# Where large and small tiles start in on-chip memory: pool order, a 128-byte pad, and a 192-byte shift of the swiglus' moving operand

## The chip, the core and the metric

The kernel runs on one core of a Trainium2 chip. The core has a matrix engine (TensorE, called PE in the rows; PEld is its loading of stationary operands), three other compute engines (VectorE = DVE, ScalarE = ACT, GpSimd = POOL), and a queue engine (SyncE = SP) that issues most transfers. Operands lie in SBUF, 128 partitions wide; "address" below means the byte offset inside a partition, which is the same in all of them. Matmul results go to PSUM banks. The metric is device microseconds (us) of one execution, less is better.

## What is computed

The reference is two transformer blocks of two layers each, on one sequence of 256 tokens and 1024 features, in float32. Cut to what the change touches:

```python
def swiglu(h, w_gate, w_up, w_down):
    return (jax.nn.silu(h @ w_gate) * (h @ w_up)) @ w_down

def first_block(x, mem, ...):                      # D_MODEL 1024, D_FF 2816, SEQ 256
    for layer in range(2):
        x = x + 0.5 * swiglu(rms_norm(x, ...), ...)
        x = x + (diff_stickbreak_mixer if layer == 0 else mla_mixer)(rms_norm(x, ...), ...)
        x = x + memory_cross_attention(rms_norm(x, ...), rms_norm(mem, ...), ...)
        x = x + 0.5 * swiglu(rms_norm(x, ...), ...)
    return x

def second_block(x, ...):                          # FFN_HIDDEN 2816
    for l in range(2):
        x = _layer_norm(ALPHA * x + mixers(x) @ w_out[l], ...)
        x = _layer_norm(ALPHA * x + swiglu(x, ...), ...)
    return x
```

So there are six swiglus, and they hold most of the weights.

## The kernel before, in words

**Three products for one.** Every large matrix product is done in split precision. `parted` (lines 144 to 159) takes a weight tile of 128 x 1024 floats that SP has brought to `wr`; ACT writes its rounded part `wh` (line 157), DVE the rest `wl` (line 158). Activations are split the same way into `op` (high) and `ol` (low) by `split_T` (lines 232, 233) or inside `swiglu` (lines 348, 349). A product is then wl·op + wh·ol + wh·op: three matmuls, each with a stationary operand of 128 columns of its own.

**The swiglu.** `norm_T` transposes the normalised x into tiles made by `operand(8)`: 8 blocks of 128 features, each 256 tokens wide, 4 blocks to a tile of 1024 floats, two `op` and two `ol` tiles. In the gate and up part (11 turns of 4 weight tiles of 24 matmuls: 1056 matmuls, recorded under line 467) the weights are stationary and the activations move, 256 columns a time. The product of gate and up goes to 22 further blocks (six `op` and six `ol` tiles). In the down part (`dense`, lines 195 to 219, matmuls recorded under 215, 216 and 217) the activations are stationary, 128 columns a time, and the weights move, 512 columns a time: 2 halves of 11 weight tiles of 12 matmuls, 264 in all. The last four weight tiles of the second half do not use the kept `wh` and `wl` but eight tiles of the scope, so that they can be split early (`apart`).

**Scopes and pools.** The program is a sequence of scopes: ffn, m0 (first mixer and memory attention), ffn, ffn, m1, ffn, m2, ffn2, m2, ffn2. `KEEP` tiles (`x`, `wr`, `wh`, `wl` and small gains) live through the whole program. For each scope, `SCOPES` lists tags with the number of their buffers; `scope` opens one pool for each tag in the order of the list, and the pools are laid one behind the other in SBUF. A tile of tag `s` or `ls` (any suffix) is 16 floats, 64 bytes; `b05` is 512 bytes, `b1` 1024, `b2` 2048, and `op`, `ol`, `g4`, `wh`, `wl` are 4096. So the order of the list sets every address, and the number of 64-byte tiles ahead of a large one sets where it starts within 512 bytes. The next scope lies on the same memory as the last one; a tile of it waits for the readers and writers of just those old tiles that it covers.

**Order of the work.** The instructions of an engine are put in order at build time by a scheduler that goes by priorities and by when an operand's room is free; on the chip each engine takes them in that order, and so does the SP queue. Work of the next scope (`later(-ahead)` in `norm_T`) may be moved ahead of the end of the last, as far as its room is free by then.

**m2's own projections** (`dense_T`, line 1035) are written like a swiglu's gate and up part: stationary weight slices of 128 columns from the kept `wh` and `wl`, 256 moving columns from `op` and `ol`, the same three products, recorded under line 467 too.

Of the kernel before, what the change touches and what calls it, by code (L numbers as in the profile page):

```python
# [14 lines left out]
F32 = mybir.dt.float32  # L15
F32R = mybir.dt.float32r
# [4 lines left out]
X = mybir.AxisListType.X  # L21
# [7 lines left out]
class Core:  # L29
# [4 lines left out]

    KEEP = dict(x=2, g1=4, v1=1, wr=4, wh=3, wl=2)
    SCOPES = {
        "ffn": (dict(s=10, ls=16, g4=2, b2=6, b1=6, b05=2, lb1=1, op=8, ol=8, wh=4, wl=4),
                dict(t=2, d=6)),
        "ffn2": (dict(s=10, ls=8, b2=6, b1=6, op=8, ol=8, wh=4, wl=4, g2=4),
                dict(t=3, d=5)),  # L40
        "m0": (dict(s=8, ls=10, g4=2, b2=6, lb4=4, lb2=7, lb8=1, b1=1, b05=1, chains=4, b2C0=3, sC0=4, b2C1=3, sC1=4, olK=2, sC2=4,
                     b2C3=3, sC3=4, sO=3, b2O=2, opK=2, b2C2=3, b2K=3, sK=8, lsK=2, lb2K=2, lb4K=1, op=3, ol=3),
                dict(t=1, o=1, d=2, tK="t", pC0=1, pC1=1, pC2=1, pC3=1, aC0="pC0", tC0="pC0", aC1="pC1", tC1="pC1", aC2="pC2",
                     tC2="pC2", aC3="pC3", tC3="pC3", oO="o")),
        "m1": (dict(sC2=4, ls=14, g4=2, b2=5, lb2=9, b1=3, lb4=4, lb4K=1, lb05=2, lb1=1, chains=4, b2C0=2, sC0=4, b2C1=2, sC1=3,
                     b2C2=2, s=8, b2C3=3, b05=6, sO=4, ol=4, olK=2, b2K=3, sK=8, lsK=2, lb2K=3, sC3=5, op=5, opK=2),
                dict(t=1, o=1, d=2, tK="pC0", pC0=1, pC1=1, pC2=1, pC3=1, aC0="pC0", tC0="pC0", aC1="pC1", tC1="pC1", aC2="pC2",
                     tC2="pC2", aC3="pC3", tC3="pC3", oO="o")),
        "m2": (dict(lb4R=1, s=11, op=3, ol=2, lb2N=5, lb2R0=3, lb2R1=3, b2R0=1, b2R1=1, lb4N=1, b05R=4, b05G=3, b05N=3, lb05N=2,
# [202 lines left out]
    def operand(self, nb, groups=None):  # L252


        groups = groups or [("op" + self.stream, min(4, nb - b)) for b in range(0, nb, 4)]
        V = [[self.tagged(g.replace("op", lo), dict(self.SIZES).get(g[1:3], 1024), F32R)[:, :n * 256].rearrange("p (k t) -> p k t", t=256)
              for g, n in groups] for lo in ("op", "ol")]
        at = [(i, j) for i, (g, n) in enumerate(groups) for j in range(n)]
        put = lambda h, b, m: [v[at[b][0]][:, at[b][1]:at[b][1] + m, h * 128:(h + 1) * 128] for v in V]
        get = lambda h, k: [v[at[k][0]][:, at[k][1], h * 128:(h + 1) * 128] for v in V]  # L260
        get.both = lambda k: [v[at[k][0]][:, at[k][1]] for v in V]
        get.blocks = lambda b, m: [v[at[b][0]][:, at[b][1]:at[b][1] + m] for v in V]
        return put, get
# [6 lines left out]
    def norm_T(self, xs, gain, gates=True):  # L270


        nc = self.nc
        ahead = self.AHEAD if gates else 0
        with self.later(-ahead):
            put, get = self.operand(8)
            ss = [self.t(2) for _ in range(2)]
        for i in range(2):

            with self.later(0 if i else -ahead):  # L280
                for h in range(2):
                    y = x = xs[h][:, 512 * i:512 * i + 512]
                    if gain is not None:
                        y = self.t(512)
                        nc.vector.tensor_tensor(y, x, gain[:, 512 * i:512 * i + 512], op=OP.mult)  # L285
                    self.split_T(y, 4, lambda b, m: put(h, 4 * i + b, m))
                    if gain is not None:
                        nc.scalar.activation(self.t(512), x, AF.Square, accum_out=ss[h][:, i:i + 1])
        if gain is not None:
            get.r = []  # L290
            for h in range(2):
                nc.vector.tensor_tensor(ss[h][:, :1], ss[h][:, :1], ss[h][:, 1:], op=OP.add)
                get.r.append(self.rstd(ss[h][:, :1], 1, 1.0 / 1024, 1e-6, self.l(1)))
            if gates:
                self.gate = self.pow
        return get
# [71 lines left out]
    def load_consts(self, cp):  # L368

        c = self.consts.tile([128, FIRST], F32, name="cf")  # L370
        self.nc.scalar.dma_start(c, cp[:, :FIRST])
        self.c = {k: c[:, a:a + n] for k, (a, n) in CONST_AT.items() if a < FIRST}
        self.ident = self.c["ident"]
        self.mhalf = self.c["mhalf"]
        self.ones = self.consts.tile([128, 128], F32, name="ones")
        self.nc.gpsimd.memset(self.ones, 1.0)

    def load_masks(self, cp, cb):
# [96 lines left out]
class Mix1(Core):  # L475
# [96 lines left out]
    def mixer0(self, filler):  # L572
# [23 lines left out]
        for h in range(2):  # L596
            qT["qb", h] = self.l(1024)
            self.fill(qT["qb", h], 0.0)
        V = {(n, h): self.l(512) for n in ("va", "vb") for h in range(2)}
        pair = lambda t: t.rearrange("p (b t) -> p b t", b=4)  # L600
# [32 lines left out]
        def value(n):  # L633
            return lambda h, ps: self.evac(V[n, h], ps, xT.r[h])

# [1253 lines left out]
```

## Time and profile before

| | |
|---|---|
| median of 3 runs | 2046.84 us (2044.94 to 2047.52) |
| the profiled execution, its own time | 2048.2 us |
| span of that execution in the trace | 2046.5 us |
| mean granted TensorE clock over the span | 0.989 |
| PE busy, share of the span | 1957.1 us, 96% |
| weight loads busy | 1740.0 us, 85% |
| DVE, ACT, POOL busy | 61%, 49%, 9% |
| read from HBM | 315.82 MB, 155 GB/s over the span |

Matmuls are pipelined: one lasts some 280 or 390 ns in the records, and the next starts long before it ends. What a matmul costs in a stream is therefore the step from its start to the next start, not its duration. In the stretches of the swiglus PE and PEld are busy all the time, at the full clock.

### The profile page before, as it was taken

The numbers are of one execution on the slowest core, as the hardware profiler recorded it, in microseconds if no ns is written. First come the engines' busy times: TensorE is split into PE (matmuls) and PEld (weight loads), VectorE is DVE, ScalarE is ACT, GpSimd is POOL, SyncE is SP. The second block draws the span as 40 slices with busy tenths as digits, with TensorE's granted clock in tenths as the row PEclk, the third lists the DMA queues.
The fourth block names the chain that finished last, engine by engine and source line by source line (L and its number), as shares of the span: only waits on it lengthen the run. The fifth ranks groups of instructions, "written<-read, shape, count | busy, mean of one in ns | idle before, by whom it ended". The sixth has DMA issues, their size and how long they took to land.

```text
span 2046.5 us, 34153 instructions
## 1 busy us (share of the span) xinstructions
PE 1957.1 (96%) x13548; PEld 1740.0 (85%) x13548; DVE 1257.9 (61%) x2007; ACT 1007.6 (49%) x1607; POOL 190.9 (9%) x270
## 2 busy tenths in 40 slices
PE   8999899899999998899999999998999999999998
PEld 7997678799989986777899888877998787878996
DVE  5655774666556655776666557756555667476555
ACT  4544556545444544665554445553544455444442
POOL 0000401000000000330000021311000212210000
PEclk9999899999999999999999999999999999999999
DMA  6656543456556655324466665313665655025664
GB/s 213 186 187 214 155 138 104 125 178 185 187 173 184 185 187 188 120 95 146 139 186 184 203 160 140 115 32 114 185 183 187 178 152 158 5 83 173 185 186 137
DMA packets 158640, 319.09 MB, mean 156 GB/s; under 512 B 28944, under 2 KB 49680, under 8 KB 158480
## 3 DMA queue, kind: packets, MB, share of 16 engines
q1 hardware_dynamic: 157888, 315.79, 50.2%
q8 instruction: 106, 1.74, 0.4%
q0 software_dynamic: 160, 0.52, 0.1%
q10 hardware_dynamic: 432, 0.60, 0.1%
q14 instruction: 54, 0.44, 0.1%
HBM read 315.82 MB, written 1.05 MB: 155 GB/s over the span
## 4 chain that ended last, share of the span: by engine, by line
PE 53%; DVE 3%; ACT 1%; issue 1%; DMA 1%; POOL 0%; SPq 0%; DVEq 0%; ACTq 0%; POOLq 0%
PE pd L467 23%; PE pd L216 6%; PE pd L215 6%; PE pd L217 6%; PE po L467 2%; DVE wl L158 1%; PE ppC L467 1%; PE pg L1234 1%; PE pg L467 1%; PE pr L1510 0%; PE pt L503 0%; PE pq L1510 0%; PE pq L1519 0%; PE pt L229 0%; PE pq L1515 0%
## 5 line engine op out<-in xcount | busy, mean ns | idle before, releaser
L158 DVE TENSOR_TENSOR wl<-wr,wh 128x1024 fp32r<-128x1024 f32 (+2 forms) x557 | 677.5, 1218 | 435.6 <-PE pd L467 174.6
L157 ACT ACTIVATE wh<-wr 128x1024 fp32r<-128x1024 f32 (+2 forms) x557 | 584.8, 1051 | 600.1 <-PE pd L467 291.5
L467 PE MATMUL pd<-op,wl 128*128 128x256 f32 x2320 | 656.2, 283 | 8.3 <-DVE lb2R L1310 4.5
L467 PE MATMUL pd<-ol,wh 128*128 128x256 f32 x2320 | 656.1, 283 | 0.4 <-DVE ol L233 0.3
L467 PE MATMUL pd<-op,wh 128*128 128x256 f32 x2320 | 653.9, 282 | 0.0
L467 PEld LDWEIGHTS pd<-op,wl 128*128 128x128 f32 x2320 | 438.7, 189 | 10.4 <-DVE lb2R L1310 5.0
L467 PEld LDWEIGHTS pd<-ol,wh 128*128 128x128 f32 x2320 | 439.4, 189 | 1.6 <-DVE ol L233 0.8
L467 PEld LDWEIGHTS pd<-op,wh 128*128 128x128 f32 x2320 | 439.7, 190 | 0.7 <-issue 0.7
L216 PE MATMUL pd<-wl,op 128*128 128x512 f32 (+5 forms) x984 | 378.5, 385 | 4.3 <-DVE wl L158 4.1
L217 PE MATMUL pd<-wh,op 128*128 128x512 f32 (+5 forms) x984 | 375.3, 382 | 0.0
L215 PE MATMUL pd<-wh,ol 128*128 128x512 f32 (+5 forms) x984 | 357.7, 386 | 2.8 <-DVE ol L233 1.7
L216 PEld LDWEIGHTS pd<-wl,op 128*128 128x128 f32 x984 | 186.4, 189 | 41.4 <-DVE wl L158 6.6
L215 PEld LDWEIGHTS pd<-wh,ol 128*128 128x128 f32 x984 | 185.5, 189 | 39.4 <-DVE ol L233 1.9
L217 PEld LDWEIGHTS pd<-wh,op 128*128 128x128 f32 x984 | 186.4, 189 | 35.3
L242 POOL TENSOR_TENSOR ls<-s,cf 128x1 f32<-128x1 f32 (+2 forms) x30 | 25.6, 857 | 760.6 <-DVE s L241 565.7
L345 DVE TENSOR_TENSOR b<-pd,b 128x256 f32<-128x256 f32 x132 | 56.0, 424 | 63.7 <-ACT b L344 44.0
L242 POOL TENSOR_TENSOR s<-s,cf 128x1 f32<-128x1 f32 (+2 forms) x22 | 22.3, 1017 | 444.8 <-DVE s L241 443.4
L344 ACT ACTIVATE b<-b 128x256 f32<-128x256 f32 x88 | 36.7, 417 | 46.3 <-DVE b L343 46.2
L349 DVE TENSOR_TENSOR ol<-b,op 128x512 fp32r<-128x512 f32 x66 | 45.4, 687 | 18.0 <-ACT op L348 18.0
L348 ACT ACTIVATE op<-b 128x512 fp32r<-128x512 f32 x66 | 41.7, 631 | 21.3 <-DVE b L345 20.8
L229 PE MATMUL pt<-cf,b 128*128 128x128 f32 x140 | 24.9, 310 | 26.3 <-DVE b L285 19.2
L343 DVE TENSOR_TENSOR b<-pd,lb 128x256 f32<-128x256 f32 x88 | 37.1, 421 | 16.5 <-PE pd L467 16.5
(505 smaller groups left out, 2055.8 us busy)
## 6 DMA issues: line engine op xcount, KB each, us to landing
wr<-in_ffn_gu_dram SPq DMA_DIRECT2D x264, 512.0 KB, 3.7
wr<-in_ffn_w_down_dram SPq DMA_DIRECT2D x132, 512.0 KB, 3.5
wr<-in_w_in_dram SPq DMA_DIRECT2D x45, 512.0 KB, 4.4
wr<-in_ab_w_in_dram SPq DMA_DIRECT2D x24, 512.0 KB, 3.9
wr<-in_xm_w_kv_dram SPq DMA_DIRECT2D x16, 512.0 KB, 3.5
wr<-in_w_out_dram SPq DMA_DIRECT2D x16, 512.0 KB, 3.7
wr<-in_ab_w_out_dram SPq DMA_DIRECT2D x8, 512.0 KB, 3.5
wr<-in_xm_w_q_dram SPq DMA_DIRECT2D x8, 512.0 KB, 3.9
```

The lines of the kernel that those rows point to most:

```text
L157: nc.scalar.activation(hi, raw, AF.Copy)
L158: nc.vector.tensor_tensor(lo, raw, hi.bitcast(F32), op=OP.subtract)
L215: nc.tensor.matmul(o, xl, wh[:, k], start=first, stop=False)
L216: nc.tensor.matmul(o, xh, wl[:, k], start=False, stop=False)
L217: nc.tensor.matmul(o, xh, wh[:, k], start=False, stop=last)
L242: self.pow = nc.gpsimd.tensor_tensor(r, a, self.mhalf[:, :n], op=OP.pow)
L343: nc.vector.tensor_tensor(s, ps[:, :256], R, op=OP.mult)
L344: nc.scalar.activation(s, s, AF.Silu)
L345: nc.vector.tensor_tensor(y[:, b * 256:b * 256 + 256], ps[:, 256:], s, op=OP.mult)
L348: nc.scalar.activation(hi, yv, AF.Copy)
L349: nc.vector.tensor_tensor(lo, yv, hi.bitcast(F32), op=OP.subtract)
L467: i = self.k.nc.tensor.matmul(out, lhsT, rhs, start=start, stop=stop, skip_group_check=skip)
```

## The change

It touches only where tiles lie. In the `SCOPES` of ffn, ffn2, m0 and m1 the 64-byte tags (`s...`, `ls...`) go to the end of the list; m2's list stays as it is. The constant tile `ones` is declared 128 bytes longer, so that everything behind it moves up by 128 bytes. The two `op` and two `ol` tiles of `norm_T` in ffn and ffn2 get tags of their own, `opX` and `olX`, 4608 bytes long, and their data starts 192 bytes behind the tile's start; the `op` and `ol` counts go from 8 to 6, so the number of buffers in use is as before.

```diff
     SCOPES = {
-        "ffn": (dict(s=10, ls=16, g4=2, b2=6, b1=6, b05=2, lb1=1, op=8, ol=8, wh=4, wl=4),
+        "ffn": (dict(g4=2, b2=6, b1=6, b05=2, lb1=1, opX=2, olX=2, op=6, ol=6, wh=4, wl=4, s=10, ls=16),
                 dict(t=2, d=6)),
-        "ffn2": (dict(s=10, ls=8, b2=6, b1=6, op=8, ol=8, wh=4, wl=4, g2=4),
+        "ffn2": (dict(b2=6, b1=6, opX=2, olX=2, op=6, ol=6, wh=4, wl=4, g2=4, s=10, ls=8),
                 dict(t=3, d=5)),
-        "m0": (dict(s=8, ls=10, g4=2, b2=6, lb4=4, lb2=7, lb8=1, b1=1, b05=1, chains=4, b2C0=3, sC0=4, b2C1=3, sC1=4, olK=2, sC2=4,
-                     b2C3=3, sC3=4, sO=3, b2O=2, opK=2, b2C2=3, b2K=3, sK=8, lsK=2, lb2K=2, lb4K=1, op=3, ol=3),
+        "m0": (dict(g4=2, b2=6, lb4=4, lb2=7, lb8=1, b1=1, b05=1, chains=4, b2C0=3, b2C1=3, olK=2, b2C3=3, b2O=2, opK=2, b2C2=3,
+                     b2K=3, lb2K=2, lb4K=1, op=3, ol=3, s=8, ls=10, sC0=4, sC1=4, sC2=4, sC3=4, sO=3, sK=8, lsK=2),
                 dict(t=1, o=1, d=2, tK="t", pC0=1, pC1=1, pC2=1, pC3=1, aC0="pC0", tC0="pC0", aC1="pC1", tC1="pC1", aC2="pC2",
                      tC2="pC2", aC3="pC3", tC3="pC3", oO="o")),
-        "m1": (dict(sC2=4, ls=14, g4=2, b2=5, lb2=9, b1=3, lb4=4, lb4K=1, lb05=2, lb1=1, chains=4, b2C0=2, sC0=4, b2C1=2, sC1=3,
-                     b2C2=2, s=8, b2C3=3, b05=6, sO=4, ol=4, olK=2, b2K=3, sK=8, lsK=2, lb2K=3, sC3=5, op=5, opK=2),
+        "m1": (dict(g4=2, b2=5, lb2=9, b1=3, lb4=4, lb4K=1, lb05=2, lb1=1, chains=4, b2C0=2, b2C1=2, b2C2=2, b2C3=3, b05=6, ol=4,
+                     olK=2, b2K=3, lb2K=3, op=5, opK=2, sC2=4, ls=14, sC0=4, sC1=3, s=8, sO=4, sK=8, lsK=2, sC3=5),
                 dict(t=1, o=1, d=2, tK="pC0", pC0=1, pC1=1, pC2=1, pC3=1, aC0="pC0", tC0="pC0", aC1="pC1", tC1="pC1", aC2="pC2",
                      tC2="pC2", aC3="pC3", tC3="pC3", oO="o")),
...
-        V = [[self.tagged(g.replace("op", lo), dict(self.SIZES).get(g[1:3], 1024), F32R)[:, :n * 256].rearrange("p (k t) -> p k t", t=256)
-              for g, n in groups] for lo in ("op", "ol")]
+        def room(tag, n):
+
+            at = 48 if tag[2:] == "X" else 0
+            t = self.tagged(tag, 1152 if at else dict(self.SIZES).get(tag[1:3], 1024), F32R)
+            return t[:, at:at + n * 256].rearrange("p (k t) -> p k t", t=256)
+        V = [[room(g.replace("op", lo), n) for g, n in groups] for lo in ("op", "ol")]
...
-            put, get = self.operand(8)
+            put, get = self.operand(8, [("opX", 4)] * 2 if "opX" in self.caps[0] else None)
...
-        self.ones = self.consts.tile([128, 128], F32, name="ones")
+        self.ones = self.consts.tile([128, 160], F32, name="ones")[:, :128]
```

Where operands start, as the built programs place them, in bytes within 512. "Apart" means moving start minus stationary start within 512. Slices step by 512 bytes or its multiples, so a tile's start holds for all its slices.

| matmuls | moving before | stationary before | apart before | moving after | stationary after | apart after |
|---|---|---|---|---|---|---|
| swiglus, gate and up | 0 | 384 | 128 | 192 | 0 | 192 |
| swiglus, down, kept weights | 384 | 0 | 384 | 0 | 0 | 0 |
| swiglus, down, the last four tiles | 0 | 0 | 0 | 0 | 0 | 0 |
| m2's projections (`dense_T`) | 64 | 384 | 192 | 192 | 0 | 192 |

The engines' instructions are the same in kind and number, but at the seams between scopes some stand elsewhere, since another old tile lies below. On the SP queue this is the load of the mixer's gain (`mix_norm`, 128 x 512 twice), which m0's first multiplication (line 285) needs. Near the program's start, before:

```order
L139 DMA wr_286<-in_ffn_gu_dram 128x1024
L171 DMA cp<-in_constants_dram 128x802
L171 DMA cb<-in_masks_dram 128x1608
L139 DMA wr_338<-in_ffn_gu_dram 128x1024
L139 DMA wr_368<-in_ffn_gu_dram 128x1024
```

and at the end of the first swiglu, where m0's first weights (`ab_w_in`) and the memory input are loaded, before:

```order
L132 DMA wr_2472<-in_ab_w_in_dram 128x2x512
L132 DMA wr_2490<-in_ab_w_in_dram 128x2x512
L798 DMA lb_303_2192<-in_mem_dram 128x1024
L798 DMA lb_304_2194<-in_mem_dram 128x1024
L171 DMA g_305_2196<-in_mix_norm_dram 128x512 x2
L171 DMA g_328_2259<-in_xm_mem_norm_dram 128x512 x2
```

In the changed program the load stands at the first of these places:

```order
L139 DMA wr_292<-in_ffn_gu_dram 128x1024
L171 DMA cp<-in_constants_dram 128x802
L171 DMA cb<-in_masks_dram 128x1608
L171 DMA g_305_2204<-in_mix_norm_dram 128x512 x2
L139 DMA wr_344<-in_ffn_gu_dram 128x1024
L139 DMA wr_374<-in_ffn_gu_dram 128x1024
```

It moved from behind the memory loads to the head of the program. For m1 the same load moves from the end of the third swiglu to its beginning.

On PE the place is the end of the first swiglu. Its last matmuls (here `wh_2016`, `wl_2017`), m0's first transposes (line 229, four to a row, of a gained block `b`) and m0's first projection (`ol_2201`), before:

```order
L215 MATMUL pd_1869<-wh_2016,ol_193 128x512
L216 MATMUL pd_1869<-wl_2017,op_187 128x512
L217 MATMUL pd_1869<-wh_2016,op_187 128x512
L229 MATMUL pt_2207<-cf,b_312_2205 128x128 x4
L229 MATMUL pt_2218<-cf,b_315_2216 128x128 x4
L215 MATMUL pd_2348<-wh_2352,ol_2201 128x512
L216 MATMUL pd_2348<-wl_2353,op_2199 128x512
```

In the changed program, 118 matmuls earlier:

```order
L215 MATMUL pd_1874<-wh_1896,ol_194 128x512
L215 MATMUL pd_1875<-wh_1896,ol_194 128x512
L229 MATMUL pt_2215<-cf,b_312_2213 128x128 x4
L216 MATMUL pd_1874<-wl_1897,op_188 128x512
L217 MATMUL pd_1874<-wh_1896,op_188 128x512
```

and at the swiglu's end:

```order
L215 MATMUL pd_1875<-wh_2022,ol_199 128x512
L216 MATMUL pd_1875<-wl_2023,op_193 128x512
L217 MATMUL pd_1875<-wh_2022,op_193 128x512
L229 MATMUL pt_2226<-cf,b_315_2224 128x128 x4
L215 MATMUL pd_2356<-wh_2360,ol_2209 128x512
L216 MATMUL pd_2356<-wl_2361,op_2207 128x512
```

The first four transposes moved in among the down matmuls; the second four stayed at the end. The end of the third swiglu, ahead of m1, reads alike. The split of the first four (line 232 on ACT, into an `op` tile of m0) has its new room on top of one of the `wl` tiles of the swiglu's last four weight tiles, and waits for a matmul next to the swiglu's last.

On DVE at that place the gain's multiplication of the second half of x also moves ahead, between the two updates of x (line 363 before, 368 in the changed file; line 285 before, 290 after). Before:

```order
L363 SCALAR_TENSOR_TENSOR x_65<-pd_1868,ls_178,x_65 128x512
L363 SCALAR_TENSOR_TENSOR x_66<-pd_1869,ls_179,x_66 128x512
L285 TENSOR_TENSOR b_312_2205<-x_65,g_305_2196 128x512
L285 TENSOR_TENSOR b_315_2216<-x_66,g_305_2196 128x512
L285 TENSOR_TENSOR b_318_2227<-x_65,g_305_2196 128x512
L285 TENSOR_TENSOR b_321_2238<-x_66,g_305_2196 128x512
```

and in the changed program:

```order
L368 SCALAR_TENSOR_TENSOR x_65<-pd_1874,ls_184,x_65 128x512
L290 TENSOR_TENSOR b_318_2235<-x_65,g_305_2204 128x512
L297 TENSOR_TENSOR s_2211<-s_2211 128x1
L241 TENSOR_SCALAR s_2259<-s_2211 128x1
L368 SCALAR_TENSOR_TENSOR x_66<-pd_1875,ls_185,x_66 128x512
L290 TENSOR_TENSOR b_321_2246<-x_66,g_305_2204 128x512
L233 TENSOR_TENSOR ol_2209<-pt_2215,op_2207 128x4x128
```

The multiplications of the first half (b_312, b_315) have moved some 15 instructions further up.

## Rows read from the trace of the kernel before

**Rows 1.** Page, parts 1 and 4: busy time of PE; chain that ended last.

```profile
span 2046.5 us, 34153 instructions
PE 1957.1 (96%) x13548; PEld 1740.0 (85%) x13548; DVE 1257.9 (61%) x2007; ACT 1007.6 (49%) x1607; POOL 190.9 (9%) x270
...
PE 53%; DVE 3%; ACT 1%; issue 1%; DMA 1%; POOL 0%; SPq 0%; DVEq 0%; ACTq 0%; POOLq 0%
```

**Rows 2.** Page, part 5: one of three groups of line 467 (count; busy, mean ns).

```profile
L467 PE MATMUL pd<-op,wl 128*128 128x256 f32 x2320 | 656.2, 283 | 8.3 <-DVE lb2R L1310 4.5
```

**Rows 3.** Windows in gate and up parts: us; busy (x) by engine; PEclk, DMA share, GB/s.

```profile
1005.40:1124.60 119.20, 119.20 (x1007) 119.20 (x1006) 72.42 (x94) 60.24 (x75) 0.00 (x0) 1.00 0.60 182
1422.70:1548.20 125.50, 125.50 (x1048) 125.50 (x1048) 66.84 (x74) 60.17 (x75) 0.00 (x0) 1.00 0.58 177
```

**Rows 4.** Timeline of PE in a gate and up part, first and last rows.

```profile
1049.82 0.28 PE L467 MATMUL pd<-ol,wh 128*128 128x256 f32 x1
...
1060.49 0.28 PE L467 MATMUL pd<-ol,wh 128*128 128x256 f32 x1
```

**Rows 5.** Timeline of PE in m2's projections, first and last rows.

```profile
1213.58 0.28 PE L467 MATMUL pd<-ol,wh 128*128 128x256 f32 x1
...
1224.13 0.28 PE L467 MATMUL pd<-ol,wh 128*128 128x256 f32 x1
```

**Rows 6.** Timeline of PE in the first down part, kept weights, first and last rows.

```profile
149.70 0.39 PE L216 MATMUL pd<-wl,op 128*128 128x512 f32 x1
...
160.39 0.40 PE L216 MATMUL pd<-wl,op 128*128 128x512 f32 x1
```

**Rows 7.** The same, on the last four weight tiles; then that stretch's window.

```profile
192.45 0.40 PE L217 MATMUL pd<-wh,op 128*128 128x512 f32 x1
...
203.11 0.39 PE L216 MATMUL pd<-wl,op 128*128 128x512 f32 x1
...
192.70:203.30 10.60, 10.60 (x48) 8.81 (x47) 4.42 (x4) 5.24 (x10) 0.00 (x0) 1.00 0.86 288
```

**Rows 8.** Timeline of all engines where the first swiglu ends and m0 begins.

```profile
203.34 0.39 PE L217 MATMUL pd<-wh,op 128*128 128x512 f32 x1
...
203.77 0.75 DVE L363 SCALAR_TENSOR_TENSOR x<-pd,ls,x 128x512 f32<-128x512 f32 x1 [4.69 <-PE pd L217]
204.58 0.80 SPq L171 DMA_DIRECT2D g<-in_mix_norm_dram  x2
...
208.42 2.54 DVE L285 TENSOR_TENSOR b<-x,g 128x512 f32<-128x512 f32 x4 [3.90 <-DMA g<-in_mix_norm_dram]
...
209.26 1.09 PE L229 MATMUL pt<-cf,b 128*128 128x128 f32 x4 [5.53 <-DVE b L285]
...
210.38 0.60 ACT L232 ACTIVATE op<-pt 128x512 fp32r<-128x512 f32 x1 [5.05 <-PE pt L229]
...
211.21 0.68 DVE L233 TENSOR_TENSOR ol<-pt,op 128x512 fp32r<-128x512 f32 x1
...
211.94 1.11 PE L229 MATMUL pt<-cf,b 128*128 128x128 f32 x4 [1.60 <-DVE ol L233]
...
212.71 0.77 PE L215 MATMUL pd<-wh,ol 128*128 128x512 f32 x1
```

**Rows 9.** Timeline of PE where the third swiglu ends and m1 begins.

```profile
795.92 0.39 PE L217 MATMUL pd<-wh,op 128*128 128x512 f32 x1
801.53 1.09 PE L229 MATMUL pt<-cf,b 128*128 128x128 f32 x4 [5.22 <-DVE b L285]
804.03 1.11 PE L229 MATMUL pt<-cf,b 128*128 128x128 f32 x4 [1.41 <-DVE s L241]
804.80 0.77 PE L215 MATMUL pd<-wh,ol 128*128 128x512 f32 x1
```

**Rows 10.** Windows behind those two seams (columns as in rows 3).

```profile
207.50:217.70 10.20, 6.84 (x20) 5.40 (x21) 7.58 (x26) 3.81 (x7) 5.06 (x5) 0.50 0.50 148
801.40:808.20 6.80, 5.26 (x16) 4.20 (x17) 5.22 (x12) 3.13 (x8) 1.11 (x3) 0.50 0.39 121
```

## Prediction

> **What bounds the kernel now.** I read the page first. PE is busy for 96% of the span, and the chain that ended last is mostly PE's own work; no other engine holds more than 3% of it [rows 1]. A kernel like this gets faster only if PE's stream gets denser, so the second question is what a matmul costs in it. Durations don't tell: one of line 467 lasts 283 ns [rows 2], but they overlap. I take steps from start to start.
>
> In a gate and up part the windows show PE busy all the time at the full clock, DVE for 72.4 of 119.2 us and ACT for 60.2 [rows 3]. Nothing is waited for there, so the step is PE's own pace. In the timeline 91 matmuls start from 1049.82 to 1060.49 us: 10.67 us in 90 steps, 118.6 ns [rows 4]. One of the six parts goes slower, 1048 matmuls in 125.5 us; less the two still running at its start that is 120.0 ns [rows 3]. The mean of the six is (5 x 118.6 + 120.0) / 6 = 118.8 ns.
>
> m2's projections are the comparison that this argument rests on: same line, same shape, same three products, weights from the same kept tiles, and splits by ACT and DVE at the same time. There 94 matmuls start from 1213.58 to 1224.13 us: 10.55 us in 93 steps, **113.4 ns** [rows 5]. What differs, by the table of addresses, is how far apart the two operands start: 128 bytes in a swiglu, 192 in m2.
>
> The down part has such a pair too. With kept weights 47 matmuls start from 149.70 to 160.39 us: 10.69 us in 46 steps, 232.4 ns [rows 6]. On the last four tiles, whose two operands both start at 0, 48 start from 192.45 to 203.11 us: 10.66 in 47 steps, 226.8 ns [rows 7]. This pair is less clean, as the last tiles' weights are split ahead of their turn.
>
> Then the seams. Where the first swiglu ends, PE stands idle 5.53 us and, after four transposes, 1.60 us more [rows 8]. The releaser of the first wait is DVE's multiplication by the gain, and that one had waited 3.90 us for the gain's load, which SP issued only at 204.58 us. The third swiglu ends in the same way, with 5.22 and 1.41 us [rows 9]. Behind each seam the granted clock is 0.50, the lower level of 1.2 GHz [rows 10].
>
> **The change part by part.**
>
> *Gate and up, 192 apart.* All 6 x 1056 = 6336 matmuls (of the 3 x 2320 of line 467 [rows 2]; the other 624 are m2's) get m2's distance. At m2's step they gain 118.8 - 113.4 = 5.4 ns each: 6336 x 5.4 = **34.2 us**. The bounds: nothing, if the distance isn't the cause; and on the other side a loss as large, as no row shows a moving operand at 192 over weights at 0. I take the whole gain, because the row of the same distance is the nearest there is, and m2 keeps its pace while ACT and DVE write weights.
>
> Here a rule of the Trainium skill speaks against the change. The page SBUF — State Buffer, section "Who interferes with whom", gives PE two read ports, one for the moving operand and one for weight loads, and says that PE never waits on anyone; no place there makes an address matter. By that rule this term and the next would be nothing. The trace disagrees as far as 118.6 against 113.4 ns for one shape is to be explained, but it has not moved an operand; that is a rival below.
>
> *Down, kept weights, from 384 apart to 0.* 6 x (264 - 48) = 1296 matmuls at 232.4 - 226.8 = 5.6 ns: **7.3 us**; from nothing (the last tiles are quick for another reason) to this. I take this: ACT and DVE still work for half and for four tenths of the stretch of the last tiles [rows 7], so it is no idle chip that makes it quick. The 288 on the last tiles stay at 0 apart.
>
> *Projections of m0 and m1.* Some 550 of their 512-wide matmuls also come to 0 apart, from several distances. At most 5.6 ns each, 3 us, and little of it seen where they are broken up by other work; I take nothing. m2 keeps its distances, as its list is as it was and all of it moves by 128 bytes.
>
> *The seams.* The gain's load leaves its place behind the memory loads, where it stood in the queue until 204.58 us, for the program's start, or for the third swiglu's: a whole swiglu covers it. The first half's multiplications and the first four transposes move in among the down matmuls. What is late next: the second four transposes need the one transpose bank, which is free when the first four are split, and that split waits for a matmul next to the swiglu's last. So behind the last matmul stand on DVE, in its order, the update of x (203.77, 0.75 us), one multiplication (2.54 / 4 = 0.63) and the split (0.68): to 205.8 us; ACT's 0.60 lies beside them. Then four transposes (0.77 us from 211.94 to the next matmul), and the first projection starts at 206.6 instead of 212.71: 6.1 us [rows 8]. At m1 the last matmul ends at 795.92 + 0.39 = 796.31; with the same 2.06 us on DVE and the 0.77 the projection starts at 799.1 instead of 804.80: 5.7 us [rows 9]. Together **11.8 us**. The half clock reached 5.0 us past the first projection in m0 and 3.4 in m1 [rows 10], which cost half of these, 4.2 us. An idle time of some 2 us is left, so I leave the clock's part at nothing and keep 4.2 for the range.
>
> *At no cost.* The two moved gain loads issue in 0.80 us of SP in front of weight loads. They are covered by the four weight tiles already on the way, and without that cover they cost 0.8 us once. The two multiplications moved into the down part delay a `wl` by 0.63 us each, where DVE is busy for less than half of the time [rows 7]. Faster matmuls ask for 512 KB every 24 x 113.4 ns = 2.72 us, 193 GB/s where 182 are moved now [rows 3]; the stretch of the last four tiles moves 288 [rows 7].
>
> **The sum.** 34.2 + 7.3 + 11.8 = 53.3 us. The profiled execution took 2048.2 us (span 2046.5), so 1994.9; the median of the runs, 2046.84, lies 1.4 us below it: **1994 us**, 2.6% less.
>
> **The rivals.**
>
> 1. *Paid back behind the seams.* The first projections of m0 and m1 start early but then wait for something that was ready before, weights or tables, until the 11.8 us are gone. For it: m1 pauses again behind its first transposes [rows 9]; against it: before the swiglu ends ACT runs ten instructions and 288 GB/s come in [rows 7], more than its last tiles ask for, so that m0's first weights are on their way by then. 2048.2 - 41.5 - 1.4 = 2005 us.
> 2. *Addresses play no part*: m2 is quicker for a reason of its own (its stage has other neighbours in memory and on the engines), and so are the last four tiles. Only the seams gain: 2048.2 - 11.8 - 1.4 = 2035 us. This is what the rule of the Trainium skill's page SBUF — State Buffer would make of the change.
> 3. *Half the gain.* The distance helps but the new pair of starts does not settle to m2's step, say at 116.1 ns: 17.1 + 7.3 + 11.8 = 36.2 us, 2011 us.
> 4. *Slower.* A moving start of 192 over weights at 0 collides more than 0 over 384. The spread that rows show is 5.4 ns; put on top, 6336 x 5.4 = +34.2 us, less 7.3 and 11.8: +15.1, 2062 us. It decides from (7.3 + 11.8) us / 6336 = 3.0 ns, that is from a step of 121.8 ns in gate and up parts.
> 5. *Transfers become the bound* of gate and up parts at today's 182 GB/s. Against it stand the 288. Without the 34.2 us: 2028 us.
>
> **How the numbers follow.** Forecast 64%, rival 1 14%, rival 2 7%, rival 3 7%, rival 4 5%, rival 5 3%. A measurement of this kernel can tell about 0.2%, 4 us, from no change. All but rival 4 are faster by more; one in a hundred I leave to a draw: faster 0.94, same 0.01, slower 0.05. The likeliest case alone spans 1986 (with the clock's 4.2 and the 3 us of m0 and m1) to 2003 (without the down part's gain, and a draw). The range reaches on to rivals 1 and 3: 1985 to 2012, which leaves out the rest and the edges of the forecast, somewhat under 2 in 10.
>
> **What would show it.** In the changed profile: steps of 113 to 114 ns in gate and up parts, some 1050 matmuls in 119.2 us where 1007 are now; 227 ns in the whole down part; m2's step as before; at the two seams an idle time of some 2 us of PE that ends with DVE's split, not with the gain's load; DMA near 190 GB/s in gate and up parts. The prediction is wrong if the step there stays at 118 or more, if PE waits there for `wl` or for weight loads, or if the gaps of m0 and m1 grow by what the seams gave.

## The result and the profile after

The changed kernel takes 1988.37 us (median; 1985.36 to 1990.53) against 2047.13 us before: ratio 0.9714, 95% interval 0.9697 to 0.9731, 58.8 us less where 53 were forecast. Its profiled execution took 1985.36 us; the two profiled executions differ by 62.8 us, 4 us more than the medians.

The page of the changed kernel, parts 1, 4 and 5 (answers to [rows 1, 2]; line 467 is 473 now, and the swiglus' share of it has a group of its own):

```profile
span 1983.7 us, 34147 instructions
PE 1906.5 (96%) x13548; PEld 1698.5 (86%) x13548; DVE 1257.2 (63%) x2007; ACT 1005.7 (51%) x1607; POOL 191.4 (10%) x270
...
PE 51%; issue 4%; DVE 3%; ACT 1%; DMA 0%; SPq 0%; POOL 0%; DVEq 0%; POOLq 0%; ACTq 0%
...
L473 PE MATMUL pd<-opX,wl 128*128 128x256 f32 x2112 | 584.3, 277 | 2.2 <-DVE s L241 1.0
```

PE, with the same 13548 matmuls, is busy for 50.6 us less and, of a span that is 62.8 us shorter, idle for 12.2 us less.

The gate and up parts of the six swiglus are called parts one to six below, in their order. Windows of the changed kernel: parts four and five (answers to [rows 3]), a down part, a stretch around the seam to m0, one behind the seam to m1 (answers to [rows 10]), and m1 as a whole:

```profile
962.91:1077.04 114.13, 114.13 (x1009) 114.13 (x1008) 72.64 (x94) 59.80 (x75) 0.00 (x0) 1.00 0.63 192
1374.31:1493.65 119.34, 119.34 (x1056) 119.34 (x1054) 67.46 (x77) 60.41 (x76) 0.00 (x0) 1.00 0.62 186
1076.93:1136.67 59.74, 59.74 (x266) 49.49 (x265) 31.80 (x30) 25.27 (x25) 0.68 (x3) 1.00 0.63 211
...
190.00:199.90 9.90, 7.64 (x36) 6.08 (x36) 6.13 (x16) 4.87 (x11) 2.57 (x3) 1.00 0.59 183
...
763.30:766.70 3.40, 3.40 (x10) 2.55 (x9) 2.30 (x4) 1.13 (x4) 0.00 (x0) 0.50 0.78 247
759.20:955.90 196.70, 178.13 (x983) 143.00 (x981) 140.07 (x293) 119.63 (x255) 39.02 (x59) 0.97 0.39 118
```

A window's count includes the two or three matmuls that only touch its edges. The first holds 1007 steps: 114.13 / 1007 = 113.3 ns. All six gate and up parts run at 113.3 to 113.4. The pace is even: every step of part four's window lasts 113 to 115 ns, where before those of the same part last 115 to 122 ns, in a pattern of five steps that repeats; neither has a longer pause now and then. DMA moves 192 and 186 GB/s, and PE waits for none of it. Around m0's seam the granted clock stays at 1.00, behind m1's it is still 0.50.

Timeline of PE in the changed kernel: down with kept weights (answers to [rows 6]), gate and up ([rows 4]), m2's projections ([rows 5]), first and last rows of each:

```profile
144.67 0.39 PE L216 MATMUL pd<-wl,op 128*128 128x512 f32 x1
...
155.33 0.39 PE L217 MATMUL pd<-wh,op 128*128 128x512 f32 x1
...
1009.95 0.28 PE L473 MATMUL pd<-opX,wh 128*128 128x256 f32 x1
...
1020.49 0.28 PE L473 MATMUL pd<-opX,wh 128*128 128x256 f32 x1
...
1166.29 0.28 PE L473 MATMUL pd<-ol,wh 128*128 128x256 f32 x1
...
1176.98 0.28 PE L473 MATMUL pd<-op,wh 128*128 128x256 f32 x1
```

10.66 us in 47 steps is 226.8 ns, 10.54 in 93 is 113.3, and m2's 10.69 in 94 is 113.7, as before (113.4).

Timeline of the changed kernel at the seams to m0 (all engines; answers to [rows 8]) and to m1 (PE; [rows 9]):

```profile
195.04 0.39 PE L217 MATMUL pd<-wh,op 128*128 128x512 f32 x1
...
195.47 0.75 DVE L368 SCALAR_TENSOR_TENSOR x<-pd,ls,x 128x512 f32<-128x512 f32 x1 [3.55 <-PE pd L217]
...
196.25 0.69 DVE L290 TENSOR_TENSOR b<-x,g 128x512 f32<-128x512 f32 x1
...
196.86 0.68 DVE L233 TENSOR_TENSOR ol<-pt,op 128x512 fp32r<-128x512 f32 x1
...
197.69 0.63 PE L229 MATMUL pt<-cf,b 128*128 128x128 f32 x4 [2.26 <-DVE s L297]
...
198.07 0.48 PE L215 MATMUL pd<-wh,ol 128*128 128x512 f32 x1
...
759.19 0.39 PE L217 MATMUL pd<-wh,op 128*128 128x512 f32 x1
761.84 0.63 PE L229 MATMUL pt<-cf,b 128*128 128x128 f32 x4 [2.26 <-DVE s L297]
762.22 0.48 PE L215 MATMUL pd<-wh,ol 128*128 128x512 f32 x1
```

DVE runs update, multiplication and split in one go, 195.47 to 197.54, and the transposes follow 0.15 us later. (The profile names DVE's next instruction as releaser, L297, which the transposes don't read.) From a swiglu's last matmul to the next projection it is 3.03 us from start to start at both seams, where it was 9.37 and 8.88.

Where the time went, from starts in the two traces (us; a stage reaches from first to last start):

| stage | change | forecast |
|---|---|---|
| six gate and up parts (7.2, 7.0, 8.1, 5.5, 7.5, 4.7) | -40.0 | -34.2 |
| six down parts | -7.1 | -7.3 |
| m0, its seam included | -10.5 | -6.1 |
| m1, its seam included | -5.5 | -5.7 |
| the rest (start, the gap between swiglus 2 and 3, two m2, end) | +0.2 | 0 |

### The profile page after: what moved, and what is told of

Read it like the earlier page. It is cut to its first block, busy times and chain, and to the rows that moved or that the text cites. A ratio compares the mean times of both kernels' runs of the same rounds, so it can differ in the third digit from the quotient of the medians.

```text
span 1983.7 us, 34147 instructions
## 1 busy us (share of the span) xinstructions
PE 1906.5 (96%) x13548; PEld 1698.5 (86%) x13548; DVE 1257.2 (63%) x2007; ACT 1005.7 (51%) x1607; POOL 191.4 (10%) x270
## 4 chain that ended last, share of the span: by engine, by line
PE 51%; issue 4%; DVE 3%; ACT 1%; DMA 0%; SPq 0%; POOL 0%; DVEq 0%; POOLq 0%; ACTq 0%
PE pd L473 23%; PE pd L216 5%; PE pd L215 5%; PE pd L217 5%; PE po L473 2%; PE ppC L473 1%; DVE wl L158 1%; PE pg L1240 1%; PE pg L473 1%; PE pt L509 0%; PE pr L1516 0%; PE pq L1516 0%; PE pq L1525 0%; PE pt L229 0%; PE pq L1521 0%
## 5 line engine op out<-in xcount | busy, mean ns | idle before, releaser
L157 ACT ACTIVATE wh<-wr 128x1024 fp32r<-128x1024 f32 (+2 forms) x557 | 584.6, 1051 | 552.9 <-PE pd L473 206.9
L473 PE MATMUL pd<-opX,wl 128*128 128x256 f32 x2112 | 584.3, 277 | 2.2 <-DVE s L241 1.0
L473 PE MATMUL pd<-olX,wh 128*128 128x256 f32 x2112 | 584.4, 277 | 0.3 <-DVE olX L233 0.2
L473 PE MATMUL pd<-opX,wh 128*128 128x256 f32 x2112 | 583.7, 277 | 0.0
L473 PEld LDWEIGHTS pd<-opX,wl 128*128 128x128 f32 x2112 | 397.4, 188 | 3.1 <-ACT opX L232 2.2
L473 PEld LDWEIGHTS pd<-olX,wh 128*128 128x128 f32 x2112 | 397.8, 188 | 0.7 <-DVE olX L233 0.7
L473 PEld LDWEIGHTS pd<-opX,wh 128*128 128x128 f32 x2112 | 397.6, 188 | 0.0
L473 PE MATMUL pd<-op,wl 128*128 128x256 f32 x208 | 58.5, 281 | 5.9 <-DVE lb2R L1316 4.4
L473 PE MATMUL pd<-ol,wh 128*128 128x256 f32 x208 | 58.1, 279 | 0.0
L473 PE MATMUL pd<-op,wh 128*128 128x256 f32 x208 | 57.9, 278 | 0.0
```

Source lines behind the costliest of these rows:

```text
L157: nc.scalar.activation(hi, raw, AF.Copy)
L473: i = self.k.nc.tensor.matmul(out, lhsT, rhs, start=start, stop=stop, skip_group_check=skip)
```

## The experiments

**Is it the distance, and what is the order alone worth?** Three kernels, timed on one chip together with before (2046.93 us there). The first is before with shifted operands in its old order; moving starts at 64, weights at 384.

```diff
-  "ffn": (dict(s=10, ls=16, ..., op=8, ol=8, wh=4, wl=4),      # before
+  "ffn": (dict(s=10, ls=16, ..., opX=2, olX=2, op=6, ol=6, wh=4, wl=4),
+            at = 16 if tag[2:] == "X" else 0      # ffn2 alike, m0 and m1 as before
```

> The kernel before, with nothing moved but the two opX and two olX tiles of the swiglus, whose data starts at 64 within 512; weights stay at 384, so the distance is 192; the down part and the gain's late load stay as before. Theory D (the distance of the two starts within 512 sets the step): steps of 113.4 ns in all six gate and up parts, 6336 x 5.4 = 34 us less, up to 40 as in the changed kernel, 2007 to 2013 us; down steps 232.4; idle times of 5.2 to 5.5 us at the two seams. Theory W (weights at 384 are what costs): 118.7 ns, 2047 us. Theory O (a moving operand at 0 is what costs) expects what D does.

Measured: 2031.34 us, ratio 0.9932 (0.9916 to 0.9947). Its windows in gate and up parts two and five and in m1, and its timeline at the seam to m0:

```profile
412.17:530.77 118.60, 118.60 (x1010) 118.60 (x1008) 72.77 (x94) 60.10 (x75) 0.00 (x0) 1.00 0.60 185
1418.13:1536.81 118.68, 118.68 (x1049) 118.68 (x1048) 66.66 (x75) 60.17 (x75) 0.00 (x0) 1.00 0.62 187
...
780.40:991.40 211.00, 187.09 (x987) 148.50 (x985) 143.03 (x298) 120.16 (x256) 38.32 (x59) 0.93 0.36 112
```

```profile
202.68 0.84 PE L229 MATMUL pt<-cf,b 128*128 128x128 f32 x4 [5.08 <-DVE b L290]
...
205.32 0.90 PE L229 MATMUL pt<-cf,b 128*128 128x128 f32 x3 [1.80 <-DVE ol L233]
```

Parts one, five and six run at 113.3 ns (118.68 / 1047), two to four at 117.8 (118.60 / 1007), at one distance. So 192 is quick with other starts too, but it has **two steps**, and a part keeps the one it has for a thousand matmuls. The seams are as long as before: the old order keeps the wait for the gain. The expected 2007 to 2013 us are missed by 18 us: three parts at 117.8 cost 3 x 4.7 us, and m1 took 211.0 us at a mean clock of 0.93, 8.7 us longer than in before's profile.

The second is the changed kernel with the moving start at 128.

```diff
-            at = 48 if tag[2:] == "X" else 0
+            at = 32 if tag[2:] == "X" else 0
```

> The changed kernel with the moving operand 128 instead of 192 bytes behind a multiple of 512; weights at 0, so the distance is 128 as before the change, and no operand lies where it lay before. Theory D: 118.6 ns in gate and up parts, 2023 to 2028 us (34 to 40 more than 1988), down steps 227 and seams as in the changed kernel. Theories O (a moving start of 0 costs) and W (weights at 384 cost): 113.4 ns, 1988 us.

Measured: 2024.16 us, ratio 0.9898 (0.9878 to 0.9918). Windows in gate and up parts four and six:

```profile
980.04:1099.54 119.50, 119.50 (x1010) 119.50 (x1008) 72.69 (x94) 60.35 (x75) 0.00 (x0) 1.00 0.59 183
1828.10:1954.23 126.13, 126.13 (x1053) 126.13 (x1052) 67.35 (x76) 60.18 (x75) 0.00 (x0) 1.00 0.57 176
```

119.50 / 1007 = 118.7 ns in five parts, 126.13 / 1051 = 120.0 in the sixth: before's two steps [rows 3, 4], with weights at 0. 64 bytes of the moving start decide, and neither a moving start of 0 (theory O) nor weights at 384 (theory W) is what costs. Against the changed kernel's profile its gate and up parts are 35.1 us longer; that is the distance alone (by the medians of the runs the kernel is 35.8 us longer).

The third moves the down part's stationary operand by 128 bytes as well, so that both distances are those of before (384 on the last four weight tiles too), in the new order.

```diff
-            at = 48 if tag[2:] == "X" else 0
+            at = 32 if "opX" in self.caps[0] else 0
```

> The changed kernel with the old distances put back in the swiglus: 128 in gate and up parts, and 384 in the down part, by a start of the product's op and ol tiles 128 bytes behind a multiple of 512 (the last four weight tiles come to 384 too, 288 matmuls, some 1.6 us). Only the seams are then as changed. Theory D: gate and up 118.6, down 232.4 ns, and the time is that of before less what the seams give, 11.8 to 16 us: 2031 to 2037 us. If addresses play no part: 1988 us. If the seams gave nothing: 2047 us.

Measured: 2029.28 us, ratio 0.9924 (0.9905 to 0.9942). Windows of its fourth gate and up part and the down part behind it:

```profile
985.12:1104.62 119.50, 119.50 (x1010) 119.50 (x1008) 72.69 (x94) 60.35 (x75) 0.00 (x0) 1.00 0.59 183
1104.62:1165.96 61.34, 61.34 (x267) 49.75 (x266) 31.63 (x30) 25.37 (x25) 0.77 (x8) 1.00 0.61 205
```

61.34 / 264 = 232.3 ns. What the change holds beside the swiglus' distances (the lists, the swiglus' own tags, the pad) gives 17.7 us, somewhat more than the 11.8 to 16 expected, and its seams are short (idle 1.73 and 2.26 us). In its profile m0 is 10.4 us shorter than before, m1 5.2 and the gate and up parts 6.3, while down parts and the rest are 3 us longer. The six down parts are 8.7 us longer than in the second kernel; of their 1584 matmuls before had 1296 at this distance: 7.1 us. The whole time is only 5.1 us longer, as the second kernel's profile has 3.0 us more in what the last row of the table above counts (the rest).

**Which distances?** One kernel with another distance in each swiglu, and two more like it. The last of the three repeats 64, 320 and 448.

```diff
+    SHIFT = (0, 16, 32, 64, 96, 48)   # then (80, 112, 40, 44, 52, 56) and (112, 80, 16, 80, 112, 16); 4 bytes each
-            at = 48 if tag[2:] == "X" else 0
+            at = self.SHIFT[self.turns] if tag[2:] == "X" else 0
```

> The changed kernel with another moving start in each of the six swiglus, in order 0, 64, 128, 256, 384 and 192 bytes, weights at 0. Theory D: 118.6 ns in the third (128) and 113.4 in the sixth (192), and a step of its own in each of the others, which nothing here has shown yet; by the row of moving 384 over stationary 64 in short stretches (117 to 118 ns) a distance of 320 is between. Theory O: the first (0) is slow, the others 113.4. If no distance but 128 is slow, five of six are at 113.4 and the time is within 6 us of 1988; if no distance but 192 is quick, about 2016 us.

> Six further distances of the moving from the stationary operand in gate and up, one for each swiglu: 320, 448, 160, 176, 208 and 224 bytes. Known so far: 0 and 256 120.0 ns, 64 117.8, 128 and 384 118.7, 192 113.3 or 117.8. Theory M (distance d and 512 - d are alike, as 128 and 384 were): 320 gives 113.3 or 117.8, 448 gives 117.8. Its rival (192 stands alone): 320 and 448 at 118 to 120. Between 128 and 256: if the addresses count in steps of 64 bytes, 160 and 176 give 118.7 as 128 does, and 208 and 224 give 113.3 or 117.8 as 192 does; if the distance counts by the byte, the four lie between these and differ from one another.

> The changed kernel with the swiglus' moving operand 448, 320, 64, 320, 448 and 64 bytes behind the weights' start. Measured once each so far: 448 113.3 ns, 320 117.8, 64 117.8; 192 113.3 or 117.8. Theory Z (all odd multiples of 64 bytes are alike, each has the two steps 113.3 and 117.8): every part at one of these two, and at least one distance of the three with a step other than before. Rival V (each distance has a step of its own): 448 113.3 twice, 320 and 64 117.8 twice each.

Measured: 2022.71, 2019.97 and 2011.98 us (one run each). Windows of the first kernel at distances 0, 64 and 192, of the second at 448 and 176, of the third at 448 twice:

```profile
19.37:143.08 123.71, 123.71 (x1033) 123.71 (x1032) 73.96 (x95) 61.77 (x76) 0.00 (x0) 1.00 0.59 181
411.74:530.34 118.60, 118.60 (x1010) 118.60 (x1009) 72.79 (x94) 60.07 (x75) 0.00 (x0) 1.00 0.60 184
...
1830.32:1953.18 122.86, 122.86 (x1044) 122.86 (x1044) 66.68 (x75) 60.20 (x75) 0.00 (x0) 1.00 0.61 181
```

```profile
408.20:522.33 114.13, 114.13 (x1009) 114.13 (x1008) 72.73 (x94) 59.91 (x75) 0.00 (x0) 1.00 0.63 192
...
978.72:1098.80 120.08, 120.08 (x1009) 120.08 (x1008) 72.71 (x94) 60.54 (x75) 0.00 (x0) 1.00 0.60 182
```

```profile
18.97:140.40 121.43, 121.43 (x1033) 121.43 (x1032) 73.91 (x95) 61.04 (x76) 0.00 (x0) 1.00 0.61 184
...
1396.66:1515.54 118.88, 118.88 (x1050) 118.88 (x1050) 66.72 (x76) 60.18 (x75) 0.00 (x0) 1.00 0.63 187
```

Steps from first to last start of a part, in ns, over all kernels of this study, before and after included (parts in brackets; where matmuls interrupt a part, of its longest piece):

| distance | step |
|---|---|
| 0, 256 | 120.0 (one each) |
| 128 | 118.7 (17), 120.0 (2) |
| 384 | 118.7 (1) |
| 64, 320 | 117.8 (three each) |
| 192 | 113.3 (41), 117.8 (8) |
| 448 | 113.3 (2), 117.8 (1) |
| 160, 176, 208, 224 | 117.3, 119.3, 119.2, 118.3 (one each) |

At 128 and 192, which were run with two pairs of starts each, the distance sets which steps there can be; the others were run with one pair. Counting in 64 bytes is out (208 isn't 192). Nothing shows d and 512 - d to be alike: 448 gave 113.3 in two parts of three, 64 in none of three, but three parts are few where a part can have either step. That every odd multiple of 64 has both steps holds for 192 and 448 and isn't shown for 64; at 320 only a short stretch of m2 in before has both, 12 steps of 113 to 115 ns from 1243.71 us and, after a pause, some 30 of 117 to 119.

The same for the down part, whose stationary operand moves:

```diff
+    SHIFT = (0, 16, 32, 48, 64, 80)
-            at = 48 if tag[2:] == "X" else 0
+            at = 48 if tag[2:] == "X" else self.SHIFT[self.turns] if "opX" in self.caps[0] else 0
```

> The changed kernel with the swiglus' hidden tiles, the stationary operand of the down part, 0, 64, 128, 192, 256 and 320 bytes behind a multiple of 512, one for each swiglu, so that the moving operand stands at a distance of 0, 448, 384, 320, 256 and 192. Known: 0 gives 226.8 ns, 384 gives 232.4. Theory D (the distance sets the step here too, each with its own value): at least three different steps, 226.8 at 0 and 232.4 at 384. Rival T (any two tiles that both begin at a multiple of 512 are quick, all others are slow): 226.8 at 0 and 232.4 at all five others, and the time is 1988 + 5 x 264 x 5.6 ns = 1995.4 us. Gate and up stay at distance 192: 113.3 ns, or 117.8 in some parts by theory S of the run with the changed kernel alone.

Measured: 1996.8 us (one run). Windows at distances 448, 384 (146 steps each) and 320 (264 steps):

```profile
524.54:558.60 34.06, 34.06 (x149) 27.43 (x148) 19.16 (x21) 15.23 (x19) 0.00 (x0) 1.00 0.55 185
708.17:742.10 33.93, 33.93 (x149) 27.47 (x147) 19.17 (x21) 15.21 (x19) 0.00 (x0) 1.00 0.55 187
1085.75:1146.18 60.43, 60.43 (x266) 49.56 (x265) 31.70 (x30) 25.27 (x25) 0.77 (x8) 1.00 0.63 208
```

0: 226.8, 448: 233.3, 384: 232.4, 320: 228.9, 256: 227.0, 192: 233.3 ns. The distance counts here too, with other favourites: 192, best in gate and up, is among the worst. Rival T is out by these steps; its time, 1995.4 us, came near by luck: the down parts grew by 5.1 us against the changed kernel's profile, not by 7.4, and part one ran at 117.8 ns.

**Does the kernel keep the quick step, and where do the seams come from?** On another chip (before: 2045.92 us) the changed kernel unaltered, and with the old lists of m0 and m1.

> The changed kernel once more, unaltered, on another chip. Six distances in one kernel had given 117.8 ns at distance 192, where the changed kernel's own profile had 113.3 in all six gate-and-up parts. Theory R (the quick step belongs to the kernel and its order of instructions): 113.3 ns in all six parts again and 1985 to 1991 us. Theory S (at 192 there are two steps, and each part or execution falls into one by chance): some parts at 117.8 ns, each of which costs 1056 x 4.4 ns = 4.7 us, so a time between 1988 and 2016 us that differs from chip to chip.

Measured: 1992.81 us (1985.0 to 2003.83), ratio 0.9744 (0.9696 to 0.9791). In its profile all six parts are at 113.3 ns, as theory R wants, but the runs spread beyond its 1985 to 1991 us. 6.3 of the 7.4 us over the first profile stand in m1, 203.0 us at a mean clock of 0.93 by its window, against 196.7 at 0.97 in the first. The run at 2003.83 has no trace, so whether parts ran at 117.8 ns in it stays open.

```profile
760.30:963.30 203.00, 185.55 (x982) 148.15 (x980) 140.21 (x293) 119.96 (x255) 38.95 (x58) 0.93 0.37 114
```

```diff
-  "m0": (dict(g4=2, b2=6, ..., s=8, ls=10, sC0=4, ..., lsK=2),
+  "m0": (dict(s=8, ls=10, g4=2, b2=6, lb4=4, ..., sC0=4, ...),      # as in before; m1 alike
```

> The changed kernel with the tile lists of the two attention stages m0 and m1 as they were before, so that their small tiles stand where they stood; the swiglus as changed. If the seams between a swiglu and m0 or m1 became short by the new places of m0's and m1's tiles, their idle of about 5 and 1.5 us comes back at each and the time is 1988 + 12 to 16 = 2000 to 2004 us. If they became short by the swiglus' own new list (the places that the swiglu's tiles leave free), the time stays at 1988 us. Gate-and-up 113.3 and down 226.8 ns either way.

Measured: 2003.5 us, ratio 0.9785 (0.9762 to 0.9808). By the time alone, the lists of m0 and m1 would be worth the seams; the profile says otherwise. The waits are short (idle 2.26 and 3.13 us) and m0 is 10.9 us shorter than before. Of the 18.3 us that its profile takes more than the changed kernel's, 14.7 are lost in gate and up, in parts one, five and six; here one and five with part two between them:

```profile
19.41:140.84 121.43, 121.43 (x1033) 121.43 (x1032) 73.92 (x95) 61.07 (x76) 0.00 (x0) 1.00 0.60 184
408.38:522.51 114.13, 114.13 (x1009) 114.13 (x1008) 72.64 (x94) 59.92 (x75) 0.00 (x0) 1.00 0.62 192
1383.84:1507.39 123.55, 123.55 (x1051) 123.55 (x1050) 66.82 (x76) 60.22 (x75) 0.00 (x0) 1.00 0.60 180
```

121.43 / 1031 = 117.8 and 114.13 / 1007 = 113.3. With the kernel in the old order (long seams) this puts the short seams on the swiglus' own new lists (the pad, which this kernel has too, moves all tiles alike).

**What picks the step?** In parts two to four two small matmuls (line 311 in the changed kernel) interrupt the stream 48 matmuls in (in part one 24); in the changed kernel part two ran at 117.8 ns until then and at 113.3 behind it. Two kernels put more such pairs in, a third only one each in parts one, five and six. The scheduler often parted an added pair, so that each of its two matmuls interrupts alone, with 24 matmuls of the stream between them.

```diff
+            if g == 2:      # second kernel: if g:   third: only in parts one, five and six
+                pt = self.p("t")
+                for h in range(2):
+                    nc.tensor.matmul(pt[:, h * 128:(h + 1) * 128], self.ones, self.ident, start=True, stop=True)
```

> The changed kernel with two more 128x128 matmuls of the constant tiles ones and ident into a spare bank in each swiglu, 96 matmuls in where the swiglu already has such a pair (the first four), 48 matmuls in where it has none (the last two); their result is not used. At distance 192 a gate-and-up part holds 113.3 or 117.8 ns to its end; behind such a pair it was 113.3 in 12 of 12 parts that came in at full clock (parts two to four of four kernels), and either without one (113.3 five times, 117.8 three times in parts five and six of the changed layout). Theory P (the pair sets the step): 113.3 ns behind it in all six parts, and a time of 1985 to 1990 us with little spread between runs; the pairs cost 6 x 0.36 us. Theory Q (every start is a chance of its own): the new pair draws again, some parts at 117.8, and a spread of 1988 to 2013 us as the changed kernel has (1985 to 2004).

> As the kernel with one more pair, but with a pair behind every 48 matmuls until a swiglu has had four to seven of them. Theory P (the pair sets the step): every piece of 48 behind a pair runs at 113.3 ns, 2 us more than with one pair. Theory Q (chance): some of the 48-pieces at 113.3 and some at 117.8 ns within one part. Rival T (the pairs alternate): the step changes at each pair.

> As the kernel with one more pair, but the pair only in the three parts whose step had come out either way: the first (96 matmuls in) and the last two (48 in); parts two to four keep the one pair that they have. Three pairs cost 3 x 0.6 us. Theory P (the pair sets the step at 113.3 ns, wherever it comes at full clock): 113.3 ns in all six parts behind the pair; the time is that of the changed kernel (1988 and 1993 us on two chips) plus 1.8 us at most, so 1985 to 1995, and what spread is left between runs follows the mean granted clock. Theory Q (chance): one or more of the three parts at 117.8 ns, 4.7 us each, and a spread of up to 14 us between runs of one clock. The kernel with one more pair has left this open: six parts at 113.3 ns in its profile, but 1999 to 2015 us in its runs.

Measured: 2003.1 us (1998.84 to 2014.67), ratio 0.9799 (0.9774 to 0.9824); 2021.35 us (one run); 1989.32 us (1986.91 to 1992.33), ratio 0.9720 (0.9707 to 0.9733). Windows of two pieces behind a pair of the second kernel (47 and 743 steps), of a part and of m1 in the first, of two parts in the third:

```profile
38.83:44.18 5.35, 5.35 (x49) 5.35 (x48) 3.24 (x7) 2.56 (x5) 0.00 (x0) 1.00 0.50 159
...
57.45:141.60 84.15, 84.15 (x745) 84.15 (x744) 53.19 (x69) 42.45 (x53) 0.00 (x0) 1.00 0.64 192
```

```profile
1392.59:1506.72 114.13, 114.13 (x1009) 114.13 (x1008) 64.88 (x74) 58.71 (x74) 0.00 (x0) 1.00 0.65 193
...
763.30:965.50 202.20, 182.67 (x983) 146.03 (x981) 140.58 (x293) 119.35 (x255) 40.37 (x58) 0.95 0.36 115
```

```profile
1383.19:1497.32 114.13, 114.13 (x1009) 114.13 (x1008) 64.90 (x74) 58.79 (x74) 0.00 (x0) 1.00 0.63 193
1805.61:1919.74 114.13, 114.13 (x1009) 114.13 (x1008) 64.90 (x74) 58.77 (x74) 0.00 (x0) 1.00 0.63 193
```

In the second kernel all 56 pieces of 20 or more matmuls behind a pair, or half of one, at full clock run at 113.3 to 114.1 ns from their second start on, while its fifth part ran at 117.8 until its first pair; the long pieces of all six parts of the first and of the third are at 113.3. So with the moving start at 192 and weights at 0 a pair sets the step, as theory P has it, with two exceptions at full clock. Both are pairs that began less than 0.5 us after the clock rose, and behind both the step was 117.8: in part one of the first kernel until its added pair 3 us later, and in part one of the kernel with the old lists of m0 and m1 to its end:

```profile
18.34 0.32 PE L473 MATMUL pd<-opX,wh 128*128 128x256 f32 x1
...
18.85 0.61 PE L311 MATMUL pt<-b,ones 128*128 128x128 f32 x4
```

Parts two to four of before with shifted operands, moving 64 over weights 384, were at 117.8 behind theirs, and part one, whose pair also began less than 0.5 us after the clock rose, at 113.3: which step the pair gives hangs on the layout. Nor does every interruption act like a pair. Behind the four transposes of line 229, 25 matmuls into part three, the step was the other one in all eight kernels that have only distance 192: it went from 114 to 117.8 ns in four and from 117.8 to 113.5 or 114.1 in four.

Theory P's times came true only for the third kernel. The first misses them by 13 us: in its profile m1 took 202.2 us, and its six gate and up parts together 5 us more than the changed kernel's; why four more runs reach 2014.67 no trace shows. The second took 18 us more than the first where 2 were expected: its 54 further pairs made the gate and up parts 24.1 us longer, 0.45 us a pair. No version beats the changed kernel: the third is its equal, at one pair's price for each of three parts.

## Why the prediction was right, point by point

- *Gate and up, 34.2 us*: the step went from 118.6 and 120.0 to 113.3, m2's; by the comparison with the second kernel the distance is worth 35.1 us. The parts as a whole gave 40.0. The other 4.9 the second kernel's parts, at the old distance, gave too, 4.2 of it ahead of the long stretches of parts two and three. In part three PE waited there three times before, 1.6 us in all; the second kernel and the changed one have no such wait, nor has before with shifted operands in the old order, so it went with the tiles' own tags, which all three have. In part two the first matmuls before ran at half clock (mean 0.83 from 414 to 424 us, 1.00 now). The prediction had no term for either.
- *Down, 7.3 us*: 7.1 in the profiles, and 7.1 from the step of the third kernel. The doubt that the last tiles were quick for another reason is gone.
- *Projections of m0 and m1, at nothing*: by the built programs some 700 of their 512-wide matmuls come to 0 apart, not 550. Their steps at full clock went from 230.1 to 229.2 ns in m0 and from 231.2 to 229.5 in m1, 1 us in all, so nothing was near enough.
- *The seams, 11.8 us*: the waits gave 9.37 - 3.03 = 6.3 and 8.88 - 3.03 = 5.9, together 12.2, by the steps named: update, multiplication, split, transposes. The two stages gave 16.0, as much as with the clock's 4.2 that was kept for the range. It was m0 that got more: 0.50 no longer follows its seam, while m1's still has it. Neither stage's part is a firm number, and that they add up to just 16.0 is in part luck: m0 took 211.2 us before and 207.9 in before with shifted operands, with the same long waits at the seam, and m1 took 196.7 to 203.0 us in two profiles of one kernel.
- *At no cost*: DMA at 186 to 194 GB/s in gate and up, no wait of PE for `wl` there. Rival 5 is out.
- *Rivals 1 and 4*: m0 gave back nothing, and no step of any distance came to 121.8 ns.
- *Rival 2*: out by 64 bytes of one operand's start (118.7 against 113.3 ns). The Trainium skill's page SBUF — State Buffer, section "Who interferes with whom", has PE wait on no one; the runs here show PE's pace hanging on where its own two operands lie.
- *Rival 3* stood at 7% for a step between the two. There is no half, but there is 117.8 ns, which three parts of the kernel with the old lists of m0 and m1 kept: its 2003.5 us lies between forecast and rival. The prediction took 113.4 for the distance's step; it is the better of two, and the trace of before held the other as well. Twenty of m2's projections there, with the same starts as those of [rows 5], take 117.8 ns: 2.12 us in 18 steps from the second of them to the last (timeline below). Six parts at that step would have cost 28 us, the kernel would have taken some 2016 us, and the cause would have been the same. So the mechanism was right, and that all six parts of the changed kernel had the better step in both of its profiles was luck as far as the prediction's reasons go.

```profile
1238.95 0.28 PE L467 MATMUL pd<-op,wh 128*128 128x256 f32 x1
...
1241.07 0.29 PE L467 MATMUL pd<-op,wh 128*128 128x256 f32 x1
```

## What to carry to other kernels

When two streams of the same matmul run at different paces with nothing waited for, compare where their operands start (here modulo 512 bytes, as all slices step by multiples of that), and move one by 64 bytes at a time: steps are to be measured for each shape, since 256 and 512 columns have different favourites. Look at such a step part by part and in more than one profile, because one address can have two. A list of buffers also sets who waits for whose old tile: check the order of loads and of the waits at a seam whenever it is permuted.

## What the runs showed of the hardware that was not expected

- At one distance a stream keeps one of two steps (113.3 or 117.8 ns at 192 and 448, 118.7 or 120.0 at 128) for up to a thousand matmuls, and a short interruption by other matmuls can change it: a pair gave 113.3 in one layout and 117.8 in another, four transposes the step that the stream had not had. What in the addresses makes the two steps, and why a pair right behind the clock's rise was followed each time by the step that later pairs of its layout did not give, stays open.
- m1 took 196.7 us at a mean granted clock of 0.97 and 203.0 at 0.93 in two profiles of the same kernel, more than the gain at its seam.
